# All blocks of two output projections in seven-product pairs, with the first pair's products in another order

## The chip, the cores and the metric

One NeuronCore of a Trainium2 chip runs the whole program. The time is the device time of one execution in microseconds, given as the median of several runs. The profile is one execution of the same program, taken by the hardware profiler. PE is the engine for matmuls, PEld its loading of weights, DVE the vector engine, ACT the scalar engine, POOL the general one, SP the queue that issues most of the DMAs.

## What is computed

The kernel is one inference step of a two-layer decoder for 576 tokens (512 of a prompt and 64 of eight samples) at a model width of 2048. All is float32, with each operand split into a rounded part and a rest, so that three matmuls make one product. The change concerns only the last line of each layer:

```python
def gla_layer(h, ...):          # first layer
    ...
    o = o.reshape(B, L, GLA_VALUE_DIM).astype(h.dtype) * jax.nn.silu(r)
    return h + o @ w_out, S.astype(s0.dtype)

def swa_layer(h, ...):          # second layer
    ...
    o = o.astype(h.dtype) * jax.nn.silu(z)
    return h + o @ w_out

# trunk: y = rmsnorm(h, g_final)
```

`o @ w_out` is a product of 576 x 2048 with 2048 x 2048, computed with features in the partitions and tokens in the columns.

## The kernel before

**Layout.** Activations lie in `HP[0..3]`, four rows of 128 features x 576 tokens each; `hpt(k)` is row k of 16. Before a projection they are split into `X[k]`, a rounded part and a rest of 576 columns each. The 576 columns are two halves of 288 (HT). Weights come in blocks of 128 output features x 2048 input features. They are loaded in tiles `raw` (eight groups of 128 input features, three buffers) and split in chunks of four groups into `wh` (a copy on ACT) and `wl` (a subtraction on DVE); four buffers each let the splits run up to four chunks ahead of PE (L166 to 175).

**Plain block** (`dense`, L185): 16 groups x 3 parts x 2 halves = 96 matmuls of 288 columns for one block of outputs.

**Pair** (`dense_pair`, L221): two blocks of outputs are made together. Inputs are divided into k < 8 and k >= 8, tokens into the two halves, which makes a 2 x 2 by 2 x 2 product of blocks with quarters x11, x12 (k < 8), x21, x22 (k >= 8). It is done with seven products instead of eight, by Winograd's form: 7 x 8 x 3 = 168 matmuls of 288 columns for what two plain blocks do with 192. The products are A, P4, P5, B, P6, P7, C (`PRODUCTS`, L217). Their inputs are x11, x21, x22, the differences t1 = x11 - x12 and t2, t3, t4 (`sums`, L258: t3 = x22 - x12, t2 = t3 + x11, t4 = t2 - x21, in groups g of two k each), and weights w11, w12, w22 and sums s1 to s4 of quarters. s1 and s3 are added by an accumulating DMA that POOL issues (L233); s2 and s4 are made in place from s1 on DVE (L241, L243). `pair_out` (L292) evacuates each product and puts the two output blocks together.

**Where t1 lies.** `XT` holds t2, t3, t4 in tiles of their own. t1 replaces x12: `first_sums` (L275) writes x11 - x12 over x12 in `HP`, and `split_half` (L281) splits it into the right halves of X[0..7]. A plain block needs x12 there, a pair needs t1.

**Stages.** `out_start` (L881) begins a projection: it splits all 16 rows, runs plain blocks (12 and 13 in the first layer, 12 in the second) with the last group of sums (`sums_hp(3)`) beside the first of them, then `first_sums`, and after the plain blocks the split of t1. Ahead of it the last gate blocks (`r_phase`, L376, and `z_phase`, L914) run with the groups 0 to 2 of sums beside them. X[k] is one tile for each k, so row k of the new input can be split only after the last gate block has read the old X[k]. The pairs follow: seven in the first layer, six (outputs 0 to 11) in the second.

**Tail of the second layer** (L1197 to 1253). Outputs 13, 14, 15 (`NB` = 3) are plain blocks again, in two parts of 320 and 256 columns, so that the final norm of the first part runs beside the second. They need x12 back in X: the second halves of rows 0 to 7 were stored to `dg2` by the gate phase and are read into unused rows of `HP[3]` (six) and a tile `st` (two) and split after the last pair. After each part come the sum of squares, the norm (`make_rstd`, `rstd_soon`), sixteen scalings on DVE (L1252) and sixteen stores (L1253).

**Order.** The kernel is built with `TileContext(nc, schedule_with_timeline_sim=True)` (L1359). The builder fixes the order of each engine's queue, with what stands earlier in the program first among what it takes to be ready. On the chip each queue runs in that order.

## Time and profile before

| | us |
|---|---|
| median of 3 runs (1757.25 to 1759.37) | 1758.03 |
| the profiled execution, its time | 1753.48 |
| the profiled execution, its span | 1751.70 |

| engine | busy us | share of the span |
|---|---|---|
| PE | 1729.3 | 99% |
| DVE | 1274.6 | 73% |
| ACT | 852.2 | 49% |
| POOL | 137.6 | 8% |

The share of busy time is an average over stages with different limits. What a change of one stage is worth is read in that stage: when its blocks end, and which engine is late. A row of the timeline is one instruction, or several of one kind that follow one another.

### The profile page before, as it was taken

How to read it: one execution, taken by the hardware profiler on the slowest of the kernel's cores; microseconds unless marked ns; L12 is line 12 of the kernel's file. 1: busy time of each engine (PE TensorE's matmuls, PEld its weight loads, DVE VectorE, ACT ScalarE, POOL GpSimd, SP SyncE). 2: the span in 40 equal slices, each digit the busy share in tenths (PEclk: the TensorE clock that was granted, in tenths of full speed). 3: DMA queues.
4: the chain of work that ended last, by engine and by line, in shares of the span. 5: the costliest groups of instructions: out<-in, count | busy, mean ns of one | idle time of the engine just before them, and what ended most of it. 6: DMA issues, size and time to landing. Idle time of an engine off the chain costs nothing.

```text
span 1751.7 us, 33967 instructions
## 1 busy us (share of the span) xinstructions
PE 1729.3 (99%) x12862; PEld 1709.6 (98%) x12862; DVE 1274.6 (73%) x2895; ACT 852.2 (49%) x1773; POOL 137.6 (8%) x216
## 2 busy tenths in 40 slices
PE   9999999999999999999999999999999999999997
PEld 9999999999999999999999999999999999999996
DVE  8567776777777787658777866787878755587774
ACT  7543334334334443435444655677767632364441
POOL 3000001001001000100121100100101000002210
PEclk9999999999999999999999999999999999999998
DMA  8345644565465344522677444343333252227643
GB/s 313 110 150 180 199 139 125 170 188 155 149 184 183 117 135 151 167 96 86 190 218 209 158 138 112 95 126 94 113 94 103 71 168 88 85 92 196 191 149 108
DMA packets 127123, 253.86 MB, mean 145 GB/s; under 512 B 23120, under 2 KB 52688, under 8 KB 126928
## 3 DMA queue, kind: packets, MB, share of 16 engines
q1 hardware_dynamic: 123216, 238.06, 42.9%
q0 software_dynamic: 3744, 13.63, 4.3%
q8 instruction: 101, 1.65, 0.4%
q14 instruction: 62, 0.51, 0.1%
HBM read 196.20 MB, written 44.83 MB: 138 GB/s over the span
## 4 chain that ended last, share of the span: by engine, by line
PE 93%; issue 2%; DMA 2%; DVE 2%; ACT 1%; SPq 0%; POOL 0%; POOLq 0%; DVEq 0%; ACTq 0%
PE pd L181 59%; PE pb L251 16%; PE pb L661 2%; PE pb L1076 1%; PE pb L747 1%; PE pd L469 1%; PE pb L836 1%; PE pb L1059 1%; PE pb L835 1%; PE pb L833 1%; PE pb L1058 1%; PE pb L748 1%; PE pb L1086 1%; PE pb L1087 1%; PE pb L679 1%
## 5 line engine op out<-in xcount | busy, mean ns | idle before, releaser
L181 PE MATMUL pd<-x,wh 128*128 128x288 f32 x5376 | 982.6, 298 | 0.0
L181 PEld LDWEIGHTS pd<-x,wh 128*128 128x128 f32 x5376 | 806.2, 189 | 7.1 <-ACT wh L169 0.3
L181 PE MATMUL pd<-x,wl 128*128 128x288 f32 x2688 | 591.5, 298 | 0.0
L169 ACT CAST wh<-raw 128x512 fp32r<-128x512 f32 x422 | 260.6, 618 | 401.2 <-PE pd L181 317.7
L181 PEld LDWEIGHTS pd<-x,wl 128*128 128x128 f32 x2688 | 437.6, 189 | 2.8
L170 DVE TENSOR_TENSOR wl<-raw,wh 128x512 fp32r<-128x512 f32 x422 | 303.4, 720 | 152.5 <-ACT wh L169 150.2
L251 PE MATMUL pb<-x,wh 128*128 128x288 f32 x832 | 166.7, 295 | 0.0
L251 PEld LDWEIGHTS pb<-x,wh 128*128 128x128 f32 x832 | 133.5, 188 | 0.0
L251 PE MATMUL pb<-t,wh 128*128 128x288 f32 x624 | 125.9, 296 | 0.7 <-ACT wh L169 0.6
L251 PE MATMUL pb<-x,wl 128*128 128x288 f32 x416 | 122.3, 295 | 0.0
L170 DVE TENSOR_TENSOR wl<-rs,wh 128x512 fp32r<-128x512 f32 x104 | 81.8, 791 | 32.4 <-ACT wh L169 30.2
L169 ACT CAST wh<-rs 128x512 fp32r<-128x512 f32 x104 | 64.0, 620 | 83.5 <-PE pb L251 76.2
L251 PEld LDWEIGHTS pb<-t,wh 128*128 128x128 f32 x624 | 100.3, 188 | 1.1 <-ACT wh L169 0.9
L251 PE MATMUL pb<-t,wl 128*128 128x288 f32 x312 | 92.5, 297 | 0.5 <-DVE wl L170 0.5
L251 PEld LDWEIGHTS pb<-x,wl 128*128 128x128 f32 x416 | 78.1, 188 | 0.0
L119 POOL TENSOR_TENSOR acc<-acc,st 128x576 f32<-128x576 f32 x46 | 71.0, 1542 | 81.3 <-ACT st L114 80.3
L117 POOL COPY acc<-st 128x576 f32<-128x576 f32 x7 | 6.3, 906 | 886.1 <-ACT st L114 797.7
L1068 ACT ACTIVATE s<-s,tiny 128x257 f32<-128x257 f32 (+1 forms) x128 | 61.1, 479 | 27.7 <-DVE tiny L1065 27.3
L815 ACT CAST sh<-Si 128x512 fp32r<-128x512 f32 x64 | 39.7, 620 | 66.5 <-PE pb L835 42.1
L114 ACT ACTIVATE st<-hp 128x576 f32<-128x576 f32 (+2 forms) x66 | 43.3, 663 | 43.9 <-DVE hp L1238 26.1
L251 PEld LDWEIGHTS pb<-t,wl 128*128 128x128 f32 x312 | 58.7, 188 | 0.9 <-DVE wl L170 0.9
L1065 DVE CUSTOM_DVE_ANT_0 s<-pb,distp,sinkp 128x256 f32<-128x256 f32 (+1 forms) x128 | 52.2, 447 | 7.1 <-PE pb L1059 6.1
(281 smaller groups left out, 2466.9 us busy)
## 6 DMA issues: line engine op xcount, KB each, us to landing
raw<-in_wA_dram SPq DMA_DIRECT2D x90, 512.0 KB
raw<-in_wB_dram SPq DMA_DIRECT2D x64, 512.0 KB
Si<-in_state_dram SPq DMA_DIRECT2D x64, 256.0 KB
out_gla_sample_dram<-Si SPq DMA_DIRECT2D x64, 256.0 KB
raw<-in_wOB_dram SPq DMA_DIRECT2D x26, 512.0 KB
raw<-in_wOA_dram SPq DMA_DIRECT2D x25, 512.0 KB
rs<-in_wOA_dram SPq DMA_DIRECT2D x14, 512.0 KB
rs<-in_wOA_dram POOLq DMA_DIRECT2D x14, 512.0 KB, 8.3
```

The costliest lines, as they stand in the source:

```text
L114: act(sq[:, lo:hi], src, AF.Square)
L119: self.eng.tensor_tensor(self.acc[:, lo:hi], self.acc[:, lo:hi], sq[:, lo:hi], ALU.add)
L169: nc.scalar.copy(wh, raw)
L170: vec.tensor_tensor(wl, raw, f32(wh), ALU.subtract)
L181: mm(p[:, a, :HT], w, x[:, part, a * HT:(a + 1) * HT], start=(k == 0 and w is wh and part == 0), stop=(k == KT - 1 and w is wl))
L251: mm(p, wt[:, kk, :], xpart(x, k, part), start=(opens and k == 0 and wt is wh and part == 0), stop=(k == 7 and wt is wl), skip_group_check ...
L469: mm(held[i][a][:, :HT], w[:, k % 4, :], X[k][:, part, a * HT:(a + 1) * HT], start=(k == 0 and w is wh and part == 0), stop=(k == KT - 1 a ...
L661: mm(p[:, o:o + N], keys(li)[:, f * 128:(f + 1) * 128], queries(li)[:, f, :], start=(f == 0), stop=(f == 1))
L679: mm(p[:, 0:N], k[:, f, :], qx[:, f, 0:N], start=(f == 0), stop=(f == 1))
L815: nc.scalar.copy(sh, Si)
L1065: vec.tensor_tensor_reduce(s[:, e, off:256], p[:, e * 256 + off:(e + 1) * 256], distp[:, off:256], slope(i), sinkp[:, i:i + 1], ALU.add, A ...
L1068: act(s[:, e, off:257], s[:, e, off:257], AF.Exp, scale=-1.0, bias=tiny[:, e:e + 1], accum_out=tiny[:, 2 + e:3 + e])
```

## The change

- `split_pairs` takes the place of `out_start`. For the k < 8 it makes x11 - x12 for two rows at once in a tile `st` and splits x11 and the difference as halves of X[k]; the rows k >= 8 are split whole. Then comes the last group of sums. There are no plain blocks; `HP` keeps x12.
- The first projection is eight pairs. The second is seven pairs, in the order 12, 0, 2, 4, 6, 8, 10, and its tail has two plain blocks (14 and 15) instead of three.
- `dense_pair` takes an order of products. The first pair of each projection runs `FIRST` (A, P5, B, P4, P6, P7, C); its loads are issued in the order in which this needs them.
- x12 comes back during the last pair (10): four halves are loaded into `HP[3]` ahead of it, four into two `st` tiles after product A, and all eight are split after product B.

```diff
@@ -218,14 +218,21 @@
                 "B": ("w12", "x21", 0, False), "P6": ("s2", "t2", 3, True), "P7": ("s3", "t3", 1, True),
                 "C": ("s4", "x22", 2, False)}
 
-    def dense_pair(wdram, blk, evac):
+    ORDER = ("A", "P4", "P5", "B", "P6", "P7", "C")
+
+    FIRST = ("A", "P5", "B", "P4", "P6", "P7", "C")
+
+    def dense_pair(wdram, blk, evac, order=ORDER):
 
         def quarter(b, hf):
             return wdram[blk + b, :, hf * 1024:(hf + 1) * 1024].rearrange("p (k n) -> p k n", n=128)
 
         raw = {}
-        for name, b, hf, more in (("w11", 0, 0, None), ("w22", 1, 1, None), ("s1", 1, 0, (1, 1)),
-                                  ("w12", 0, 1, None), ("s3", 1, 0, (0, 0))):
+        parts = {"w11": (0, 0, None), "w22": (1, 1, None), "s1": (1, 0, (1, 1)), "w12": (0, 1, None), "s3": (1, 0, (0, 0))}
+        for name in (PRODUCTS[n][0] for n in order):
+            if name not in parts:
+                continue
+            b, hf, more = parts[name]
             pool, tag = (wp, "raw") if more is None else (tpool[0], "rs")
             raw[name] = pool.tile([128, 8, 128], F32, tag=tag, name=nm(tag), bufs=3)
             dma(raw[name], quarter(b, hf))
@@ -233,7 +240,8 @@
                 nc.gpsimd.dma_start(raw[name], quarter(*more), accum_op=ALU.add)
         raw["s2"] = raw["s4"] = raw["s1"]
         banks = {}
-        for n, (w, x, b, opens) in PRODUCTS.items():
+        for n in order:
+            w, x, b, opens = PRODUCTS[n]
             if opens:
                 banks[b] = bank(b)[:, 0:HT]
             p = banks[b]
@@ -271,12 +279,6 @@
     def sums_hp(g):
         i = 2 * g % 4
         return sums(g, HP[g // 2][:, i:i + 2, :], HP[g // 2 + 2][:, i:i + 2, :])
-
-    def first_sums():
-
-        for h in range(2):
-            x12 = HP[h][:, :, HT:NT]
-            vec.tensor_tensor(x12, HP[h][:, :, 0:HT], x12, ALU.subtract)
 
     def split_half(k, src):
 
@@ -324,22 +326,16 @@
                     dma(dh1[j], hpt(j))
         return f
 
-    def out_pairs(wdram, js, src, ss, store):
+    def out_pairs(wdram, js, src, ss, store, also=None):
         for j in js:
             r1, r0 = resid(src(j + 1)), resid(src(j))
-            yield from dense_pair(wdram, j, pair_out(j, r0, r1, ss, store))
-
-    def out_block(wdram, j, src, ss, store):
-        r = resid(src(j))
-
-        def f(p):
-            if j % 4 == 0:
-                new_hp(j // 4)
-            vec.tensor_tensor(halves(hpt(j)), p, r, ALU.add)
-            ss.add(hpt(j))
-            if store:
-                dma(dh1[j], hpt(j))
-        yield from dense(wdram, j, f)
+            f = pair_out(j, r0, r1, ss, store)
+
+            def g(n, p):
+                f(n, p)
+                if also and j == js[-1]:
+                    also(n)
+            yield from dense_pair(wdram, j, g, FIRST if j == js[0] and not also else ORDER)
 
     bgs = []
 
@@ -878,18 +874,22 @@
             run(phase(range(a, a + 2)))
             drain()
 
-    def out_start(wdram, blks, src, ss, store):
-
-        for k in range(KT):
+    def split_pairs():
+
+        for g in range(4):
+            t1 = st().rearrange("p (a n) -> p a n", a=2)
+            i = 2 * g % 4
+            x = HP[g // 2][:, i:i + 2, :]
+            vec.tensor_tensor(t1, x[:, :, 0:HT], x[:, :, HT:NT], ALU.subtract)
+            for i in range(2):
+                k = 2 * g + i
+                o = new_x(k)[:, :, 0:HT]
+                nc.scalar.copy(o[:, 0, :], hpt(k)[:, 0:HT])
+                vec.tensor_tensor(o[:, 1, :], hpt(k)[:, 0:HT], f32(o[:, 0, :]), ALU.subtract)
+                split_half(k, t1[:, i, :])
+        for k in range(8, KT):
             split_plain(k, hpt(k))
-        bgs.append([sums_hp(3), 0.5, 0.0])
-        for j in blks:
-            run(out_block(wdram, j, src, ss, store))
-            if j == blks[0]:
-                drain()
-                first_sums()
-        for k in range(8):
-            split_half(k, hpt(k)[:, HT:NT])
+        finish(sums_hp(3))
 
     ssB = [None]
     with tc.tile_pool(name="lp", bufs=1) as lp:
@@ -900,8 +900,8 @@
         def x_row(j):
             return xT[j * 128:(j + 1) * 128, :]
 
-        out_start(A["wOA"], (12, 13), x_row, ss, True)
-        run(out_pairs(A["wOA"], (0, 2, 4, 6, 8, 10, 14), x_row, ss, True))
+        split_pairs()
+        run(out_pairs(A["wOA"], range(0, KT, 2), x_row, ss, True))
         ssB[0] = ss.acc
 
 
@@ -1194,31 +1194,38 @@
 
 
 
-    NB, NS = 3, 12
+    NB = 2
     ss = SumSq(nc.gpsimd)
     with tc.tile_pool(name="zp", bufs=1) as zp:
         tpool[0] = zp
         with_sums(z_phase, RS)
-        out_start(A["wOB"], (12,), lambda j: dh1[j], ss, False)
-        for j in range(0, NS, 2):
-            if j == NS - 2:
-
-                back = [HP[3][:, 1 + k // 2, k % 2 * HT:(k % 2 + 1) * HT] for k in range(6)]
-                for k in range(6):
+        split_pairs()
+
+
+        back = []
+
+        def x12_back(n):
+            if n == "A":
+                for _ in range(2):
+                    t = halves(st())
+                    back.extend([t[:, 0], t[:, 1]])
+                for k in range(4, 8):
                     dma(back[k], dg2[k])
-            run(out_pairs(A["wOB"], (j,), lambda j: dh1[j], ss, False))
-        t = halves(st())
-        for k in (6, 7):
-            dma(t[:, k - 6], dg2[k])
-            back.append(t[:, k - 6])
-        for k in range(8):
-            split_half(k, back[k])
+            elif n == "B":
+                for k in range(8):
+                    split_half(k, back[k])
+
+        run(out_pairs(A["wOB"], (12, 0, 2, 4, 6, 8), lambda j: dh1[j], ss, False))
+        for k in range(4):
+            back.append(HP[3][:, 2 + k // 2, k % 2 * HT:(k % 2 + 1) * HT])
+            dma(back[k], dg2[k])
+        run(out_pairs(A["wOB"], (10,), lambda j: dh1[j], ss, False, x12_back))
         ss.eng = vec
         rf = cp.tile([128, NT], F32, name="rstdF", tag="rstd")
         mhalf = cp.tile([128, 4], F32, name="mhalf", tag="mhalf")
         nc.gpsimd.memset(mhalf, -0.5)
         W, R = {}, {}
-        for j, tag in zip(range(KT - NB, KT), ("t4", "t2", "t3")):
+        for j, tag in zip(range(KT - NB, KT), ("t4", "t2")):
             W[j] = zp.tile([128, 2, KT, 128], F32R, tag=tag, name=nm("w"))
             R[j] = zp.tile([128, NT], F32, tag="rs", name=nm("r"), bufs=3)
             for hf in range(2):
```

## Rows read from the trace of the kernel before

**Rows 1.** The page's chain that ended last, shares of the span.
```profile
PE 93%; issue 2%; DMA 2%; DVE 2%; ACT 1%; SPq 0%; POOL 0%; POOLq 0%; DVEq 0%; ACTq 0%
```

**Rows 2.** Timeline of DVE, first projection: start us, us, what [idle before <-releaser]
```profile
791.04 0.76 DVE L381 SCALAR_TENSOR_TENSOR st<-pd,rstd 128x576 f32<-128x576 f32 x1 [1.40 <-PE pd L181]
...
807.06 0.75 DVE L381 SCALAR_TENSOR_TENSOR st<-pd,rstd 128x576 f32<-128x576 f32 x1
...
829.43 0.76 DVE L338 TENSOR_TENSOR hp<-pd,ld 128x576 f32<-128x576 f32 x1 [2.08 <-PE pd L181]
...
852.13 0.45 DVE L321 TENSOR_TENSOR hp<-pb,ld 128x288 f32<-128x288 f32 x1
...
874.44 0.44 DVE L321 TENSOR_TENSOR hp<-pb,ld 128x288 f32<-128x288 f32 x1
```

**Rows 3.** Timeline of DVE, evacuations around the second projection's front.
```profile
1534.23 0.76 DVE L919 SCALAR_TENSOR_TENSOR st<-pd,rstdB 128x576 f32<-128x576 f32 x1 [1.42 <-PE pd L181]
...
1550.18 0.75 DVE L919 SCALAR_TENSOR_TENSOR st<-pd,rstdB 128x576 f32<-128x576 f32 x1
...
1584.49 0.45 DVE L321 TENSOR_TENSOR hp<-pb,ld 128x288 f32<-128x288 f32 x1
...
1606.77 0.45 DVE L321 TENSOR_TENSOR hp<-pb,ld 128x288 f32<-128x288 f32 x1
```

**Rows 4.** Busy time by stretch; columns in the first line.
```profile
core 0: us, PE busy (x) PEld busy (x) DVE busy (x) ACT busy (x) POOL busy (x), PEclk, DMA share, GB/s
778.20:791.00 12.80, 12.80 (x99) 12.80 (x98) 9.29 (x13) 4.94 (x9) 0.00 (x0) 1.00 0.26 83
791.00:803.80 12.80, 12.80 (x99) 12.80 (x98) 12.60 (x19) 11.93 (x21) 0.00 (x0) 1.00 0.24 75
803.80:816.60 12.80, 12.80 (x99) 12.80 (x98) 11.73 (x18) 4.26 (x7) 0.00 (x0) 1.00 0.28 92
...
1534.20:1547.00 12.80, 12.80 (x98) 12.80 (x98) 12.62 (x19) 11.95 (x21) 0.00 (x0) 1.00 0.23 75
1547.00:1559.80 12.80, 12.80 (x98) 12.80 (x98) 11.29 (x19) 5.87 (x11) 0.00 (x0) 1.00 0.15 50
1559.80:1571.60 11.80, 10.67 (x76) 9.99 (x76) 11.25 (x19) 6.99 (x14) 0.88 (x1) 1.00 0.37 115
...
1740.00:1752.00 12.00, 0.90 (x4) 0.61 (x3) 6.36 (x16) 0.00 (x0) 0.00 (x0) 0.50 0.51 175
```

**Rows 5.** Timeline of DVE, one row of each kind of piece.
```profile
801.11 2.76 DVE L102 TENSOR_TENSOR x<-hp,x 128x576 fp32r<-128x576 f32 x4
...
807.73 1.29 DVE L170 TENSOR_TENSOR wl<-raw,wh 128x512 fp32r<-128x512 f32 x2
...
833.90 1.23 DVE L241 TENSOR_TENSOR rs<-rs,raw 128x1024 f32<-128x1024 f32 x1
...
1562.83 1.19 DVE L285 TENSOR_TENSOR x<-hp,x 128x288 fp32r<-128x288 f32 x3
```

**Rows 6.** Timeline of PE, waits at the start of the tail.
```profile
1701.40 0.56 PE L1236 MATMUL pd<-x,w 128*128 128x320 f32 x2 [0.55 <-ACT x L284]
1702.94 19.95 PE L1236 MATMUL pd<-x,w 128*128 128x320 f32 x141 [0.98 <-DVE x L285]
```

**Rows 7.** Timeline of DVE in the tail: evacuations and scalings.
```profile
1711.76 0.49 DVE L1238 TENSOR_TENSOR hp<-pd,r 128x320 f32<-128x320 f32 x1 [2.16 <-PE pd L1236]
...
1718.80 0.49 DVE L1238 TENSOR_TENSOR hp<-pd,r 128x320 f32<-128x320 f32 x1 [5.46 <-PE pd L1236]
...
1728.08 7.49 DVE L1252 SCALAR_TENSOR_TENSOR hp<-hp,c_vecs,rstdF 128x320 f32<-128x320 f32 x16
1735.49 0.42 DVE L1238 TENSOR_TENSOR hp<-pd,r 128x256 f32<-128x256 f32 x1
1736.37 0.42 DVE L1238 TENSOR_TENSOR hp<-pd,r 128x256 f32<-128x256 f32 x1 [0.47 <-PE pd L1236]
```

**Rows 8.** Timeline of PE in the tail, right parts.
```profile
1723.03 13.30 PE L1236 MATMUL pd<-x,w 128*128 128x256 f32 x109
```

## The prediction

> **What bounds the kernel now.** I read the chain of waits first: PE holds 93% of it [rows 1], so time is won by taking matmuls away as long as PE keeps being fed, and lost wherever PE begins to wait. Then I read the rhythm of the evacuations on DVE, because each stands at the end of a block. In the first output projection the evacuation of r block 14 starts at 791.04 and that of the second plain block at 829.43, both waiting on PE: three dense blocks in 38.39 us, 12.80 us each, 0.133 us for each of 96 matmuls. From the last evacuation of one pair to that of the next is 874.44 - 852.13 = 22.31 us for 168 matmuls, the same 0.133 us [rows 2]. So PE never waits there: the two plain blocks at the front cost only their matmuls. In the second projection the rhythm is broken: from 1534.23 two dense blocks (25.60) and a first pair (22.70, as 829.43 to 852.13 in the first projection) would end at 1582.53, and the row stands at 1584.49 [rows 2, 3]. With one plain block as cover the front already loses 1.96 us. The busy times of each stretch say why: PE is busy throughout, but for 1.1 us after 1559.8, and in the 25.6 us after 791.0 DVE is busy 12.60 + 11.73 = 24.33 us, 95%, and in the 37.4 us after 1534.2 it is busy 35.16 us, 94% [rows 4]. DVE is the second limit, at these two places alone, and the plain blocks lie there as its cover. The evacuation of r block 15, whose matmuls end at 791.04 + 12.80 = 803.84, comes only at 807.06 [rows 2]: DVE is 3 us behind already.
>
> **Change, part 1: matmuls.** First projection: two plain blocks go (25.60), an eighth pair comes (22.31): **-3.29 us** [rows 2]. Second projection: the plain block at its front goes (-12.80), a seventh pair comes (+22.31), and one of three blocks in the tail goes. How much of that last is worth anything is read in the tail (part 3).
>
> **Part 2: the two fronts.** What covered DVE is gone; what DVE must do is hardly less. Prices per piece, start to start within runs of the same form: 576 wide 0.67 us (four in 2.76, each 0.76 long), a weight split 0.60 (two in 1.29), a half 0.37 (three in 1.19), the sum of weights in place 1.23 [rows 5]. From the evacuation of the last block but one to the last weight split of the first pair DVE has: two gate evacuations of three pieces (6 x 0.67 = 4.0); four differences x11 - x12 (2.7), sixteen half splits in place of eight whole ones (5.9), eight whole splits (5.4); the last group of sums (6 x 0.67 = 4.0); fifteen weight splits (9.0); two sums of weights (2.5); six evacuation pieces of the products (5 x 0.37 + 0.67 = 2.5). Sum 36.0 us. PE has a dense block and a pair for it, 12.80 + 22.31 = 35.1 us, and its last chunk (12 matmuls, 1.6 us) comes after the last split.
> First projection: without any idle DVE would be ready at 791.04 + 36.0 = 827.0, PE at 828.6; unhindered PE would end at 803.84 + 22.31 = 826.15, so it loses 2.5 us. At the 95% of this very stretch it is 791.04 + 37.9 + 1.6 = 830.5, a loss of 4.4. Second projection: 1534.23 + 38.3 (94%) + 1.6 = 1574.1 against 1547.03 + 22.31 = 1569.34, a loss of 4.8; without idle 2.5.
> Two things move this. Downwards: the four differences need only rows of HP that are long done, and DVE is idle for 3.5 of the 12.8 us before 791.0 [rows 4]; if they go there, each front loses 2.7 less. Upwards: the queues are in order and their order is fixed when the kernel is built; in the second projection such an order cost 1.96 us even under cover, and may again, so up to 6.4 and 6.8. I take 4.4 and 4.8, the values at the busy share that the rows show. The new order of the first pair's products (P4 fourth, so that t4 of the last group, the end of the longest chain of sums, comes late) doesn't change DVE's total; it decides only which product waits. Against the old order it is worth at most the time of the two products moved ahead, 2 x 24 x 0.133 = 6.4 us, and costs at least nothing; the sum above has it in.
> Loads: a pair reads seven quarters of weights where two plain blocks read four. In the stretches named DMA has room (shares 0.15 to 0.37 [rows 4]), and a weight tile of the first pair comes free when r15's splits free it, before 800, so I put the loads of w11, w12, w22 and both residuals at nothing; were that cover gone, one would cost a late product, about 1 us. On POOL's queue come two more accumulating loads in each projection; nothing but the sums of squares stands behind them: nothing.
>
> **Part 3: the tail of the second projection.** After the last pair come the plain blocks, left part (320 columns) of each, then right part (256). One left part takes 1718.80 - 1711.76 = 7.04 us [rows 7], a right one 48 x 13.30/109 = 5.9 [rows 8]. The last left part is evacuated at 1718.80; then come its norm and sixteen scalings on DVE (1728.08 to 1735.57), and behind them in DVE's queue the evacuations of right parts, at 1735.49 and, waiting for PE, at 1736.37. The end hangs on this last one. DVE is free 16.7 us after 1718.80, PE 17.6 us after it: even now they are within 0.9 us. With two blocks PE needs 2 x 5.9 + 0.3 (the norm's matmul) = 12 us there, DVE the same 16.7. So the tail gains 0.88 us behind the last left part, not 5.9, and 7.04 ahead of it. From evacuation to the end (15.3 us) nothing changes.
> To the last left part: -12.80 + 22.31 - 7.04 = **+2.47**; behind it **-0.88**; the old loss at the front goes, **-1.96**; x12's return, which now runs during the last pair, takes away the two waits of PE for its splits, 0.55 + 0.98 = **-1.53** [rows 6]. Its loads: four are issued ahead of the last pair and four behind product A, on SP's queue, ahead of the tail's weights; two of three st tiles are held for them. The first product that follows takes the third, and POOL has freed the others a product earlier. Nothing, or at most the 1.5 us again (a split late for the tail); I take 0.4.
>
> **Sum.** Fixed: -3.29 + 2.47 - 0.88 - 1.96 - 1.53 = -5.2. New waits: 4.4 + 4.8 + 0.4 = 9.6. Together **+4.4 us**, on the profiled execution (span 1751.70, time 1753.48) 1757.9. The median shown is 1758.03, 4.55 above it; I carry that over: **1762.4 us**. 0.2% is 3.5 us, about what a measurement of this kernel can tell from no change.
>
> **Rivals.** (a) *Faster:* DVE's idle time ahead of 791.0 and 1534.2 takes all differences, and PE fills what waits remain with products whose inputs are done (P6 and P4 need the last group of sums only for k = 6 and 7). For: PE mixed blocks in the tail of before. Against: those products need weight splits, which are DVE's too. With 0.6 us for each front: 1.2 - 5.2 = -4.0, **1754.0**. It decides if DVE's backlog at the pair's end is under 1 us. (b) *The differences alone go early:* 1.7 + 2.1 + 0.4 - 5.2 = -1.0, **1757.0**. (c) *The last evacuation is queued ahead of scalings that are still waiting:* the tail becomes PE's, 16.7 - 12 = 4.7 less, **1757.7**. Against: the row at 1735.49, a right part done some 6 us before the next, stands behind all sixteen. (d) *The queues' order costs as in the old second front:* 6.4 + 6.8 + 1.5 - 5.2 = +9.5, **1767.5**. (e) *TensorE's clock:* it is granted 0.50, its 1.2 GHz level, in 1740 to 1752, after PE ran out of work, and 1.00 in 1559.8 to 1571.6 with 1.1 us of waiting [rows 4]. If a front's wait brings it down, a product at half rate costs 24 x 0.133 = 3.2 more at each front, +6.4: **1768.8**. The Trainium skill (TensorE: Matmul & The Clock Gate, "Why this matters for your kernels") warns that pauses between bursts of matmuls bring the half rate back; by that rule this change is worse than its sum, and the row at 1740 agrees with it for a long pause. No row here shows a pause of 2 to 4 us.
>
> **Chances.** Forecast 0.42 (its own range 1759.5 to 1765.5), a 0.11, b 0.25, c 0.07, d 0.09, e 0.06. Range **1755.0 to 1768.0**: it leaves out most of a, e and the upper end of d. Faster by over 0.2% (below 1754.5): 0.11. Slower (above 1761.5): two thirds of the forecast, d, e and a little of b: 0.46. Within: 0.43.
>
> **What would show it.** Right: PE has waits of 2 us and more in all within the first pair of each projection, released by DVE or ACT (weight splits, differences, t4), and DVE at 95% from 791 on; the first pair's last evacuation stands near 831 and 1574.5 instead of 826.5 and 1569.7; later pairs keep 22.31; in the tail DVE runs its sixteen scalings straight into the last evacuation, without a wait on PE, 16.7 us behind the last left part. Wrong: the first pairs last under 24 us; the differences stand ahead of 791; or the last evacuation still waits on PE. The granted clock under 1.00 in a first pair would speak for e.

## The result, and the profile after

| | us |
|---|---|
| kernel before, median of 4 (1756.80 to 1759.37) | 1757.64 |
| changed kernel, median of 4 (1767.47 to 1770.91) | 1768.37 |
| ratio, 95% interval | 1.0070 (1.0058 to 1.0081) |
| changed kernel, the profiled execution: time, span | 1770.91, 1769.1 |

By the medians the change costs 10.7 us, by the ratio 12.3 (10.2 to 14.2), where +4.4 was forecast. The direction is the forecast one, the size is more than double, and the time lies 0.4 us above the upper end of the range.

The page's busy times and its chain of the changed kernel hardly differ from those of before [rows 1]:

```profile
PE 1731.0 (98%) x12814; PEld 1709.4 (97%) x12814; DVE 1285.8 (73%) x2924; ACT 856.6 (48%) x1786; POOL 140.6 (8%) x221
...
PE 93%; DVE 2%; issue 2%; DMA 2%; ACT 0%; SPq 0%; POOL 0%; POOLq 0%; DVEq 0%; ACTq 0%
```

These shares say nothing of the loss; it has to be read in the rhythm of the evacuations. DVE's timeline of the changed kernel, first front (L377 and L381 are the first and the last piece of a gate evacuation, L883 a difference x11 - x12, L287 the rest of a half split, L323 the last evacuation of a pair):

```profile
794.28 0.76 DVE L377 SCALAR_TENSOR_TENSOR st<-pd,rstd 128x576 f32<-128x576 f32 x1 [1.40 <-PE pd L181]
...
807.75 0.75 DVE L377 SCALAR_TENSOR_TENSOR st<-pd,rstd 128x576 f32<-128x576 f32 x1
...
809.01 0.75 DVE L883 TENSOR_TENSOR st<-hp 128x576 f32<-128x576 f32 x1
...
813.42 0.81 DVE L381 SCALAR_TENSOR_TENSOR hp<-hp,c_vecs,st 128x576 f32<-128x576 f32 x1
814.15 2.09 DVE L883 TENSOR_TENSOR st<-hp 128x576 f32<-128x576 f32 x3
816.16 0.76 DVE L102 TENSOR_TENSOR x<-hp,x 128x576 fp32r<-128x576 f32 x1
816.83 2.30 DVE L287 TENSOR_TENSOR x<-st,x 128x288 fp32r<-128x288 f32 x6
...
860.94 0.45 DVE L323 TENSOR_TENSOR hp<-pb,ld 128x288 f32<-128x288 f32 x1
```

and the second front, where L919 and L923 are the pieces of the gate evacuation:

```profile
1545.26 0.76 DVE L919 SCALAR_TENSOR_TENSOR st<-pd,rstdB 128x576 f32<-128x576 f32 x1 [1.42 <-PE pd L181]
...
1559.98 0.76 DVE L883 TENSOR_TENSOR st<-hp 128x576 f32<-128x576 f32 x1
...
1564.40 0.75 DVE L923 TENSOR_TENSOR hp<-hp,st 128x576 f32<-128x576 f32 x1
1565.07 2.09 DVE L883 TENSOR_TENSOR st<-hp 128x576 f32<-128x576 f32 x3
...
1611.87 0.45 DVE L323 TENSOR_TENSOR hp<-pb,ld 128x288 f32<-128x288 f32 x1
```

From the evacuation of gate block 14 to the last one of the second pair lie one dense block (12.80), a first pair (22.70) and a pair (22.31): 57.81 us if PE never waits [rows 2]. What a kernel needs beyond that is called its **front loss** from here on. It is 860.94 - 794.28 - 57.81 = **8.85 us** in the first projection and 1611.87 - 1545.26 - 57.81 = **8.80 us** in the second. The forecast had 4.4 and 4.8. The rows say where: the first difference starts at 809.01, the other three at 814.15, directly behind the last piece of gate block 15's evacuation. These differences are `t1`, which P5, the second product in the new order, reads. PE's timeline shows that it waits for these pieces one after the other:

```profile
811.17 0.40 PE L259 MATMUL pb<-x,wh 128*128 128x288 f32 x1 [0.96 <-ACT x L286]
...
813.20 0.40 PE L259 MATMUL pb<-x,wh 128*128 128x288 f32 x1 [1.63 <-DVE x L287]
...
815.42 0.61 PE L259 MATMUL pb<-x,wh 128*128 128x288 f32 x1 [1.05 <-ACT x L286]
...
817.34 0.61 PE L259 MATMUL pb<-x,wh 128*128 128x288 f32 x1 [1.30 <-DVE x L287]
```

Busy times by stretch (columns as in [rows 4]) show what else happens there:

```profile
807.10:819.90 12.80, 7.86 (x41) 6.74 (x40) 12.80 (x24) 6.65 (x16) 0.00 (x0) 0.76 0.13 41
810.00:813.00 3.00, 0.60 (x3) 0.19 (x1) 3.00 (x5) 1.28 (x3) 0.00 (x0) 1.00 0.10 27
813.00:816.00 3.00, 1.75 (x6) 1.12 (x6) 3.00 (x6) 1.73 (x5) 0.00 (x0) 0.61 0.46 147
816.00:819.00 3.00, 1.70 (x8) 1.67 (x8) 3.00 (x8) 1.56 (x6) 0.00 (x0) 0.50 0.00 0
819.00:822.00 3.00, 3.00 (x19) 3.00 (x19) 2.83 (x5) 1.07 (x2) 0.00 (x0) 0.75 0.03 5
```

In these 12.80 us DVE has no idle time at all, and PE is idle for 4.94 us. Behind the first two of the four waits the granted clock falls: it is 0.61 in 813 to 816, 0.50, the 1.2 GHz level, in 816 to 819, and 0.75 in 819 to 822.

The tail, DVE and then PE (L1245 evacuations, L1259 scalings), to be laid beside [rows 7]:

```profile
1737.09 0.49 DVE L1245 TENSOR_TENSOR hp<-pd,r 128x320 f32<-128x320 f32 x1 [5.45 <-PE pd L1243]
...
1746.37 7.49 DVE L1259 SCALAR_TENSOR_TENSOR hp<-hp,c_vecs,rstdF 128x320 f32<-128x320 f32 x16
1753.78 0.42 DVE L1245 TENSOR_TENSOR hp<-pd,r 128x256 f32<-128x256 f32 x1
...
1754.76 1.01 PE L149 MATMUL pb<-ones,st 128*128 128x1 f32 x4 [5.47 <-ACT st L1250]
```

From the last left part to the last evacuation it takes 1753.78 - 1737.09 = 16.69 us, with the evacuation straight behind the scalings and PE without work: as forecast.

**Where the time came from.** From gate block 14 of the first projection to that of the second: 750.98 us here, 743.19 before [rows 2, 3], +7.79. Of this -3.29 are matmuls and +8.85 the front loss; 2.2 are left; they lie between the projection's last pair and gate block 14 of the second projection, in stages that the change doesn't touch (as do the 3.2 us by which 794.28 is later than 791.04, ahead of the first projection). From gate block 14 of the second to the last evacuation: 208.52 here, 202.14 before [rows 3, 7], +6.38. That is +8.80 - 1.96 (the old loss) + 2.47 - 0.88, and -2.05, a remainder, which is put down to x12's return. The changed stretches alone make 7.79 - 2.2 + 6.38 = **+11.9 us**, which the interval of the ratio holds.

### The profile page after: what moved, and what is told of

Read it like the earlier page. It is cut to its first block, busy times and chain, and to the rows that moved or that the text cites. A ratio compares the mean times of both kernels' runs of the same rounds, so it can differ in the third digit from the quotient of the medians.

```text
span 1769.1 us, 33949 instructions
## 1 busy us (share of the span) xinstructions
PE 1731.0 (98%) x12814; PEld 1709.4 (97%) x12814; DVE 1285.8 (73%) x2924; ACT 856.6 (48%) x1786; POOL 140.6 (8%) x221
## 4 chain that ended last, share of the span: by engine, by line
PE 93%; DVE 2%; issue 2%; DMA 2%; ACT 0%; SPq 0%; POOL 0%; POOLq 0%; DVEq 0%; ACTq 0%
PE pd L181 57%; PE pb L259 18%; PE pb L657 2%; PE pd L465 2%; PE pb L1076 1%; PE pb L743 1%; PE pb L1059 1%; PE pb L829 1%; PE pb L1058 1%; PE pb L832 1%; PE pb L744 1%; PE pb L831 1%; PE pb L1086 1%; PE pb L1087 1%; PE pb L465 1%
## 5 line engine op out<-in xcount | busy, mean ns | idle before, releaser
L181 PE MATMUL pd<-x,wh 128*128 128x288 f32 x5184 | 949.9, 299 | 0.0
L181 PEld LDWEIGHTS pd<-x,wh 128*128 128x128 f32 x5184 | 778.6, 189 | 7.1 <-ACT wh L169 0.3
L181 PE MATMUL pd<-x,wl 128*128 128x288 f32 x2592 | 571.3, 298 | 0.0
L181 PEld LDWEIGHTS pd<-x,wl 128*128 128x128 f32 x2592 | 422.7, 189 | 2.8
L259 PE MATMUL pb<-x,wh 128*128 128x288 f32 x960 | 197.0, 300 | 9.8 <-DVE x L287 5.8
L259 PEld LDWEIGHTS pb<-x,wh 128*128 128x128 f32 x960 | 156.6, 191 | 12.4 <-DVE x L287 6.9
L259 PE MATMUL pb<-t,wh 128*128 128x288 f32 x720 | 144.5, 296 | 0.0
L259 PE MATMUL pb<-x,wl 128*128 128x288 f32 x480 | 142.9, 299 | 1.0 <-DVE wl L170 1.0
L259 PEld LDWEIGHTS pb<-t,wh 128*128 128x128 f32 x720 | 115.6, 188 | 0.0
L259 PE MATMUL pb<-t,wl 128*128 128x288 f32 x360 | 106.2, 297 | 0.0
```

What stands on the lines that cost most here:

```text
L181: mm(p[:, a, :HT], w, x[:, part, a * HT:(a + 1) * HT], start=(k == 0 and w is wh and part == 0), stop=(k == KT - 1 and w is wl))
L259: mm(p, wt[:, kk, :], xpart(x, k, part), start=(opens and k == 0 and wt is wh and part == 0), stop=(k == 7 and wt is wl), skip_group_check ...
```

## The experiments

The front losses of all kernels are read in the same way, from the evacuation of gate block 14 to the last one of the second pair. "Sum" is the forecast's fixed part (-5.2; -3.29 and -1.9 where one projection is changed) and the losses; "measured" is the ratio's excess with its interval, in us. Each loss is read from one profiled execution. Of the edits only the main lines are shown; `...` marks what is left out.

| kernel | front 1 | loss | front 2 | loss | sum | measured |
|---|---|---|---|---|---|---|
| changed kernel | 794.28 to 860.94 | 8.85 | 1545.26 to 1611.87 | 8.80 | +12.5 | +12.3 (10.2 to 14.2) |
| differences in place | 793.15 to 855.75 | 4.79 | 1538.09 to 1601.77 | 5.87 | +5.5 | +3.7 (1.9 to 5.6) |
| with filler matmuls | 793.33 to 859.14 | 8.00 | 1540.74 to 1606.33 | 7.78 | +10.6 | +10.4 (7.7 to 13.2) |
| first projection only | 792.41 to 860.30 | 10.08 | as before | | +6.8 | +7.4 (4.7 to 10.0) |
| second projection only | as before | | 1534.98 to 1602.36 | 9.57 | +7.7 | +6.7 (4.6 to 8.8) |
| old order of products | 795.53 to 862.10 | 8.76 | 1547.95 to 1613.93 | 8.17 | +11.7 | +13.7 (10.7 to 16.8) |
| in place, fewer rests | 790.86 to 851.28 | 2.61 | 1534.68 to 1594.36 | 1.87 | -0.7 | +0.9 (-0.9 to 2.6) |
| in place, rests on GpSimd | 791.46 to 857.64 | 8.37 | 1540.20 to 1606.57 | 8.56 | +11.7 | +12.5 (10.2 to 14.9) |

Every sum lies inside its interval, so the losses account for the time. The same first front, with DVE's pieces in the same order, lost 8.85 us in the changed kernel and 10.08 in the run with the first projection only; the second front lost 8.80 and 9.57. So a difference of 1 us between two of these losses needs a reason seen in the rows. Two theories stood at the start. **S**: the differences stand too late, because each needs an `st` tile; there are three, the last gate block's evacuation takes two of them, and the differences queue behind it. **D**: as the prediction had it, DVE's total sets the loss, wherever the pieces stand. The clock was a third.

**Differences in place.** Groups 0 to 2 are written over x12 (nothing reads it any more once their sums are done), so they need no `st` tile; group 3 still does.

```diff
-            t1 = st().rearrange("p (a n) -> p a n", a=2)
             i = 2 * g % 4
             x = HP[g // 2][:, i:i + 2, :]
+            t1 = x[:, :, HT:NT] if g < 3 else st().rearrange("p (a n) -> p a n", a=2)
```

> The changed kernel, but the differences x11 - x12 of groups 0 to 2 are written over x12 in HP, so they need no st tile; only group 3 still takes one. Theory S (in the changed kernel the differences wait for an st tile that the evacuation of the last gate block gets first): the differences now run before that evacuation, the waits of PE in product P5 of both first pairs (0.96 + 1.63 + 1.05 + 1.30 us and 0.97 + 1.62 + 0.96 + 1.30 us) all but go, the granted clock stays at 1.00 there, and each front loses about 2 us instead of 8.8: 1755 to 1758. Theory D (DVE's whole work in the front decides, wherever the differences stand): only the 2.7 us of differences per front move, each front still loses 4 to 5 us: 1761 to 1764.

Measured: 1760.26 us (10 runs) against 1756.03, ratio 1.0021 (1.0011 to 1.0032), an excess of 3.7 us. Both expectations were reckoned from 1757.6 (as +5.5 and 1763.2 are below); as excesses they are +3.4 to +6.4 for D and -2.6 to +0.4 for S, so the time is D's. DVE's timeline (first two rows below), a stretch of the busy times and PE's timeline of this kernel:

```profile
784.84 0.75 DVE L883 TENSOR_TENSOR hp<-hp 128x576 f32<-128x576 f32 x1
...
809.54 0.74 DVE L883 TENSOR_TENSOR st<-hp 128x576 f32<-128x576 f32 x1
...
805.90:818.70 12.80, 11.29 (x81) 10.60 (x80) 12.73 (x21) 6.33 (x13) 0.00 (x0) 1.00 0.23 72
...
813.34 0.40 PE L259 MATMUL pb<-t,wl 128*128 128x288 f32 x1 [1.32 <-DVE wl L170]
```

The differences without a tile run ahead of gate block 14's evacuation (793.15; the row at 784.84 is the last of the three); only the fourth waits. PE has 11.29 busy of 12.80 us where it had 7.86, the clock stays at 1.00, and its longest wait at each front is now for a weight split (1.32 and 1.48 us), DVE's last and largest item. The same pieces in another place are worth 4.06 us at the first front and 2.93 at the second, the half clock included: S explains that part, and the fourth difference, which still needs a tile, is its control. The rows don't show why the differences weren't put into 798 to 807 in the changed kernel, between the evacuations of gate blocks 14 and 15, when neither held a tile; only that those which need none stand early. What is left, 4.79 and 5.87, looks like the prediction's 4.4 and 4.8 but is more than D: three of four differences (2.0 us) are out of the front now, and D's own sum without them is about 2.4 and 2.8. At the second front 1568 to 1574, where the clock is granted at 0.77 around waits of 0.28 us for a group of sums and 1.48 us for a weight split, has a share in it. More buffers for `st`, the direct test of S, were not tried.

**Filler matmuls.** The changed kernel with 34 matmuls into an unused bank ahead of P5's pieces in each first pair, so that PE isn't idle there. On PE's queue they stand as 27 ahead of P5's first matmul and 7 behind it.

```diff
+                        fill = {(0, 0): 7, (0, 1): 11, (2, 0): 7, (2, 1): 9}.get((k, part), 0)
+                        if order is FIRST and n == "P5" and wt is wh and fill:
+                            if k == 0 and part == 0:
+                                spare = bank(3)[:, 0:HT]
+                            for _ in range(fill):
+                                mm(spare, XT["t3"][:, 0, 0, 0:128], X[0][:, 0, 0:HT], start=True, stop=True)
```

> The changed kernel with 34 further matmuls of 288 columns, whose result nobody reads, in front of product P5's first matmuls of each first pair (27 ahead of the first, 7 before its second), 4.5 us at full clock, in a time in which PE waits anyway. Theory C (PE's pause brings the clock to half, and part of the front's loss is that half clock): the granted clock stays at 1.00, the waits stay as sums, and each front gives back about 3 us although PE has more to do: 1761 to 1764. Rival (the waits alone make the loss, the low clock falls into time that DVE needs anyway): no change, 1767 to 1770, or worse by what fillers delay.

Measured: 1765.66 us (4 runs) against 1756.03, ratio 1.0059 (1.0044 to 1.0075). Busy times and PE's one long wait in the first front of this kernel:

```profile
806.00:812.00 6.00, 6.00 (x47) 6.00 (x46) 6.00 (x10) 3.04 (x7) 0.00 (x0) 1.00 0.06 17
812.00:818.00 6.00, 4.49 (x33) 4.15 (x32) 6.00 (x13) 3.25 (x9) 0.00 (x0) 1.00 0.22 73
...
816.38 0.40 PE L265 MATMUL pb<-x,wh 128*128 128x288 f32 x1 [1.51 <-DVE x L293]
```

The clock is granted in full at both fronts, and the losses fall only from 8.85 and 8.80 to 8.00 and 7.78. The last wait for a half of `t1` ends just as far behind gate block 14 as in the changed kernel (23.05 us against 23.06, 22.97 against 22.99 at the second front), so the fillers delay nothing there, and the half clock of the changed kernel's trace is worth about 0.85 and 1.0 us. By the times alone the two kernels can't be told apart: +10.4 (7.7 to 13.2) and +12.3 (10.2 to 14.2).

**One projection at a time.** The first as changed and the second as before, and the other way round.

> Only the first projection is changed (eight pairs, new front); the second is that of the kernel before, with its plain block, six pairs and three tail blocks. By the rhythm in the two profiles the first projection costs 8.8 us of front loss against 3.3 us of matmuls saved: +5.5, 1763.2. If the difference between the two kernels came from elsewhere (the second projection alone, or stages that the change does not touch), it would be 1757.6 or 1754.3.

Measured: 1762.45 us (5 runs) against 1756.03, ratio 1.0042 (1.0027 to 1.0057). Its front lost 10.08 us where the changed kernel's lost 8.85. The busy times of this kernel say why:

```profile
817.00:820.00 3.00, 3.00 (x15) 3.00 (x14) 2.82 (x5) 1.20 (x3) 0.00 (x0) 0.50 0.03 5
```

The last wait for `t1` ends 23.06 us behind gate block 14 here too, but then the clock stays at 0.50 for a stretch in which PE is busy all the time: 15 matmuls in 3.00 us, where the changed kernel got through 19 at 0.75 in 819 to 822. Set against the run with fillers, the half clock cost 2.1 us in this trace, and 1.8 in the second front of the run below.

> The first projection as in the kernel before, the second as changed: the complement of the run with the first projection only. By the changed kernel's trace its front loses 8.8 us; with the fixed terms of the second projection (+2.47 - 0.88 - 1.96 - 1.53 = -1.9) this gives +6.9 us on the kernel before, and a front loss of 8 to 9 us. If the two projections hurt each other (a slower clock or a later queue carried from the first to the second), it is less: +4 or under, with a front loss under 7 us.

Measured: 1761.91 us (7 runs) against 1755.05, ratio 1.0038 (1.0026 to 1.0050). The two excesses add up to 0.0080, the whole change has 0.0070 (0.0058 to 0.0081) and, in the run with the old order below, 0.0078: no carrying over from one projection into the other shows; with these intervals one of under some 4 us would not.

**Old order of products.** The changed kernel with A, P4, P5, B, P6, P7, C in the first pairs too.

```diff
-            yield from dense_pair(wdram, j, g, FIRST if j == js[0] and not also else ORDER)
+            yield from dense_pair(wdram, j, g, ORDER)
```

> The changed kernel with the first pairs in the order of the kernel before (A, P4, P5, B, P6, P7, C) and nothing else undone. It measures what the reordering is worth. The prediction gave it between 0 and 6.4 us a front (two products of 24 matmuls moved ahead). Theory W (the queue order of PE is planned by what is ready, so products mix and the written order matters little): within 1.5 us of the changed kernel, that is +10 to +12 us on the kernel before. Theory O (P4 stands in front of P5 and B on PE and waits for the last group of sums, done at 827 in the changed kernel): each front loses 3 to 6 us more, so +16 to +23 us on the kernel before, with a wait of PE of over 4 us in a row released by DVE's sums (t).

Measured: 1768.38 us (4 runs) against 1754.64, ratio 1.0078 (1.0061 to 1.0096). PE's timeline of its first front has one long wait where the changed kernel has four shorter ones, for the same splits:

```profile
815.54 0.40 PE L259 MATMUL pb<-x,wh 128*128 128x288 f32 x1 [0.88 <-ACT x L286]
...
819.19 0.50 PE L259 MATMUL pb<-x,wh 128*128 128x288 f32 x1 [3.25 <-DVE x L287]
...
830.42 0.41 PE L259 MATMUL pb<-t,wh 128*128 128x288 f32 x1 [0.69 <-DVE t L276]
```

The losses, 8.76 and 8.17, are those of the new order, where theory O had 3 to 6 us more for each; the time, +13.7 (10.7 to 16.8), lies between the two theories and can't decide. By the losses the reordering is worth nothing that these runs can tell: theory W. P4 doesn't stand in the way: the part of it whose sums are done (18 matmuls with `t`, 811.29 to 813.69) runs ahead of P5, the rest behind, and the last group of sums costs only 0.69 us of waiting.

**In place, with 5.4 us less for DVE.** The differences in place, and the rests of rows k >= 8 aren't made: this run leaves them out, and the matmuls that read them take the rounded parts.

```diff
         for k in range(8, KT):
-            split_plain(k, hpt(k))
+            nc.scalar.copy(new_x(k)[:, 0, :], hpt(k))
...
```

> As the run with differences in place, with 8 DVE instructions less at each front: the rests of rows k >= 8 are not made (the matmuls that read them in pairs and tail read the rounded parts instead, so that PE has the same work). It leaves out that part of the computation. 8 x 0.67 = 5.4 us of DVE go at each front. Theory D (with the differences early, DVE's total sets what is left of the loss, 4.8 and 5.9 us): both losses go to 0.5 or less, the run is 8 to 10 us below the run with differences in place, about 5 us below the kernel before. Rival O (what is left is the order of the queues and the chain of the last gate block): the losses stay over 3 us each, the run is less than 4 us below the run in place.

Measured: 1756.05 us (10 runs) against 1754.64, ratio 1.0005 (0.9995 to 1.0015). PE's waits in its first front, and ACT's split that ends the second of them:

```profile
810.82 0.40 PE L259 MATMUL pb<-t,wl 128*128 128x288 f32 x1 [0.57 <-DVE wl L170]
...
820.20 0.54 PE L259 MATMUL pb<-x,wh 128*128 128x288 f32 x2 [0.62 <-ACT wh L169]
...
819.53 0.62 ACT L169 CAST wh<-rs 128x512 fp32r<-128x512 f32 x1 [0.97 <-PE pb L259]
```

The losses fall from 4.79 and 5.87 to 2.61 and 1.87. Neither theory's number holds: D had 0.5 or less, its rival over 3. Of 5.4 us taken off DVE 2.2 and 4.0 come back (at the second front the half clock of the run in place goes too). So DVE's total does set a part of what is left once the differences are early. By D's sum nothing should be left here, and 2.61 and 1.87 are. The rows show where: from matmul to matmul, against the pace of 0.133 us, PE loses 0.84 us at the first of these waits, 1.20 at the second and 0.50 at 824.1, together 2.54 of the 2.61. These are waits for weight splits, and ACT itself stood idle for 0.97 us ahead of its split at 819.53 until PE released it, by its row; that would be for one of the four `wh` buffers, a second ring. No run here tests that, so the cause of this part stays open.

**The rests on GpSimd.** The differences in place; nothing is left out, GpSimd makes the rests of rows k >= 8.

```diff
-            split_plain(k, hpt(k))
+            t = new_x(k)
+            nc.scalar.copy(t[:, 0, :], hpt(k))
+            nc.gpsimd.tensor_tensor(t[:, 1, :], hpt(k), f32(t[:, 0, :]), ALU.subtract)
```

> As the run with differences in place, with the eight rests of rows k >= 8 made on GpSimd instead of DVE; nothing is left out. By theory D it takes 5.4 us off DVE at each front; if GpSimd's subtractions don't slow DVE and end before product B needs them, it comes near the run without these rests: 1751 to 1754. If GpSimd is slow (over 1.5 us for each, 12 us in all) B and the accumulating loads behind them in its queue are late: 1758 to 1764.

Measured: 1767.31 us (4 runs) against 1754.64, ratio 1.0071 (1.0058 to 1.0085): worse than both expectations, as bad as the change itself. GpSimd's timeline, DVE's beside it, and PE's:

```profile
799.43 13.85 POOL L893 TENSOR_TENSOR x<-hp,x 128x576 fp32r<-128x576 f32 x7 [61.62 <-ACT x L892]
...
805.78 1.99 DVE L883 TENSOR_TENSOR st<-hp 128x576 f32<-128x576 f32 x1
807.69 2.46 DVE L249 TENSOR_TENSOR rs<-rs,raw 128x1024 f32<-128x1024 f32 x1
810.07 1.95 DVE L380 SCALAR_TENSOR_TENSOR st<-st,st 128x576 f32<-128x576 f32 x1
811.94 1.88 DVE L170 TENSOR_TENSOR wl<-raw,wh 128x512 fp32r<-128x512 f32 x1
...
814.25 0.40 PE L259 MATMUL pb<-x,wh 128*128 128x288 f32 x1 [4.32 <-DVE x L287]
```

GpSimd subtracts at 1.98 us for each of seven. The four pieces of DVE beside it take 1.99, 2.46, 1.95 and 1.88 us where they took 0.75, 1.22, 0.75 and 0.69 in the changed kernel: 1.2 us more for each. What was taken off DVE came back as slower work. The fourth difference itself stands earlier than in the run in place, 14.32 us behind gate block 14's evacuation against 16.39, but the split of it, for which PE waits, comes 22.29 us behind it against 20.06.

**A tail of two blocks.** The kernel before with its third tail block moved to the second front (plain blocks 12 and 13 there, 14 and 15 in the tail).

```diff
-    NB, NS = 3, 12
+    NB, NS = 2, 12
...
-        out_start(A["wOB"], (12,), lambda j: dh1[j], ss, False)
+        out_start(A["wOB"], (12, 13), lambda j: dh1[j], ss, False)
...
```

> The kernel before with block 13 of the second projection moved from the tail to the front (plain blocks 12 and 13 there, six pairs, two tail blocks); the number of matmuls is the same. Theory T (behind the last left part DVE's norm and sixteen scalings decide, not PE): the moved block costs 12.8 us ahead and gives back 7.04 + 0.88 in the tail, and the front with two plain blocks loses nothing where it lost 1.96: +2.9, 1760.5, with the last evacuation 16.7 us behind the last left part and no wait on PE. Rival (a tail block is worth its matmuls): 12.8 for 12.8 and the front's 1.96 gained, 1755.7, with the last evacuation waiting for PE 12 us behind the last left part.

Measured: 1756.55 us (10 runs) against 1756.03, ratio 1.0004 (0.9994 to 1.0013). DVE's tail:

```profile
1723.35 0.49 DVE L1239 TENSOR_TENSOR hp<-pd,r 128x320 f32<-128x320 f32 x1 [2.23 <-PE pd L1237]
...
1732.63 7.49 DVE L1253 SCALAR_TENSOR_TENSOR hp<-hp,c_vecs,rstdF 128x320 f32<-128x320 f32 x16
1740.04 0.41 DVE L1239 TENSOR_TENSOR hp<-pd,r 128x256 f32<-128x256 f32 x1
```

16.69 us again behind the last left part, set by DVE: the third block's right part was worth 0.88 us there, as the prediction worked out. The total, +0.7 (-1.1 to 2.3), is lower than the theory's +2.9 and above the rival's -1.96; from gate block 14 to the last evacuation the traces have 203.64 us against 202.14, +1.5. The theory had already counted the old loss of 1.96 us. What it left out is that PE's waits at the tail's start fall from 0.55 + 0.98 us to 0.45.

**The tail's columns 192 and 384.** The run above with the narrow part first, and the norm of the second part in four pieces of columns in place of three.

```diff
-        for lo, hi in ((0, 320), (320, NT)):
+        for lo, hi in ((0, 192), (192, NT)):
...
```

> The run with a tail of two blocks (one more plain block at the second front, tail blocks 14 and 15), with the tail's columns divided 192 and 384 instead of 320 and 256. Theory T (behind the last left part DVE's norm and scalings set the end, PE has slack): the left parts shrink by 2 x 48 x 128 columns, about 5 us by 7.04 us for 320 columns; behind the last left part PE takes over, 2 x 48 matmuls of 384 columns, about 17 us against 16.7; the last sixteen scalings and stores grow by 1 to 2 us. Sum -2.5 to -3.5 us on the run with 320 and 256 columns, so 1752.5 to 1754.5 where the kernel before has 1756.0. Rival (the stores of 384 columns set the end): no gain, 1756 or more.

Measured: 1753.71 us (11 runs) against 1754.64, ratio 0.9996 (0.9987 to 1.0005). DVE's tail:

```profile
1716.08 0.36 DVE L1239 TENSOR_TENSOR hp<-pd,r 128x192 f32<-128x192 f32 x1 [3.90 <-PE pd L1237]
...
1733.07 0.56 DVE L1239 TENSOR_TENSOR hp<-pd,r 128x384 f32<-128x384 f32 x1 [1.34 <-PE pd L1237]
```

Now the last evacuation waits for PE, 16.99 us behind the last left part: the balance has tipped to PE, as expected. Counted from gate block 14, the left parts end 4.3 us sooner than in the run above; the stretch behind the last evacuation grows by 2.0 us (17.3 against 15.4): -2.1 us by the traces where -2.5 to -3.5 was expected, and no difference from the kernel before that the runs can tell.

**x12's return alone.** The kernel before with this one part: loads ahead of the last pair and behind its product A, splits behind B.

```diff
...
+        def x12_back(n):
+            if n == "A":
+                t = halves(st())
+                for k in (6, 7):
+                    dma(t[:, k - 6], dg2[k])
+                    back.append(t[:, k - 6])
+            elif n == "B":
+                for k in range(8):
+                    split_half(k, back[k])
...
```

> The kernel before with one part of the change: x12's halves are loaded and split during the last pair (six into rows of HP[3] ahead of it, two into an st tile behind product A, all eight split behind product B). The prediction gave this part -1.53 us (two waits of PE, 0.55 and 0.98) and up to +0.4 for splits or loads that come late. Theory R: both waits of PE at the start of the tail go, 1.0 to 1.5 us below the kernel before. Rival: the eight splits delay the last pair's own weight splits on DVE or ACT, or hold an st tile that the pair needs: no gain, with waits of PE of 1 us in all inside the last pair.

Measured: 1752.86 us (12 runs) against 1755.05, ratio 0.9987 (0.9976 to 0.9997). DVE's timeline, gate block 14 of the second layer and the last evacuation:

```profile
1536.65 0.76 DVE L925 SCALAR_TENSOR_TENSOR st<-pd,rstdB 128x576 f32<-128x576 f32 x1 [1.42 <-PE pd L181]
...
1736.68 0.42 DVE L1248 TENSOR_TENSOR hp<-pd,r 128x256 f32<-128x256 f32 x1 [0.46 <-PE pd L1246]
```

200.03 us against 202.14 before [rows 3, 7]: -2.1 us, more than the two waits of [rows 6]. PE doesn't wait once from the last pair to the last left part. This part of the change is a gain by itself, and the only kernel here whose interval lies below the kernel before, if narrowly: 0.13% (0.03% to 0.24%).

## Why the prediction was wrong in size

By its own steps, in the traces:

| step | forecast | trace |
|---|---|---|
| new waits, first front | +4.4 | +8.85 |
| new waits, second front | +4.8 | +8.80 |
| new wait for x12's splits | +0.4 | 0 |
| x12's waits that go | -1.53 | -2.05 |
| matmuls, old loss, two-block tail | -3.66 | -3.66 |
| sum | +4.4 | +11.9 |

- **The step that failed is part 2.** It added up DVE's pieces, 36.0 us, took 95% for the busy share, and let the pieces stand in any order. The prices held, and so did the sum; busy times of the first front (columns as in [rows 4]), the first pair's last weight split and its last evacuation in the changed kernel:

```profile
794.28:830.00 35.72, 30.78 (x212) 29.66 (x211) 33.87 (x57) 22.10 (x43) 0.00 (x0) 0.90 0.14 46
...
832.03 0.68 DVE L170 TENSOR_TENSOR wl<-rs,wh 128x512 fp32r<-128x512 f32 x1
...
838.23 0.46 DVE L323 TENSOR_TENSOR hp<-pb,ld 128x288 f32<-128x288 f32 x1
```

  DVE is busy for 33.87 of 35.72 us, 95%, and ends its last split 38.4 us behind gate block 14's evacuation, where 37.9 was forecast. But PE isn't 1.6 us behind that, as forecast: the pair's last evacuation comes 5.5 us after the split. What failed is the order. The 1.6 us rested on PE keeping up with DVE's pieces as they come, and PE had stood idle for 4.94 us in 807.1 to 819.9. The prediction said that "the four differences need only rows of HP that are long done", and that was so, but they also need a tile to be written to. Three of them came behind the last gate block's evacuation, and PE stood still for P5 while DVE did work that was needed later. The prediction looked for what the new instructions read and didn't look for where they write. Of the 8.85 and 8.80 us the place of the differences makes 4.06 and 2.93 (0.85 and 1.0 of that, by the run with fillers, through the clock), DVE's amount of work 2.2 and 4.0 of the rest, and 2.61 and 1.87 stay open. These are differences of single traces.
- **Rival (b)** had the differences go early and priced the fronts at 1.7 and 2.1. With three of four early they cost 4.79 and 5.87: going early is possible, but not enough. Rival (a), 0.6 a front, wasn't reached even with 5.4 us less for DVE to do (2.61 and 1.87).
- **Rival (d)**, an order of the queues that costs 6.4 and 6.8, is the nearest to what happened, in its time (1767.5) and in its kind. But its price came from the old second front, where PE waited 0.63 and 0.46 us for weight splits and not for the differences; the new fronts lost 8.85 and 8.80.
- **Rival (e)**, the clock: it did fall to 0.50, behind waits of 0.96 and 1.63 us with 0.60 us of PE work in 810 to 813, where the prediction spoke of one pause of 2 to 4 us. By the run with fillers it costs 0.85 and 1.0 us in the changed kernel's trace, and 2.1 and 1.8 in the runs with one projection, not 3.2: a part of the half clock lay over a stretch where PE had only 1.70 of 3.00 us to do, and that part cost nothing. The Trainium skill (TensorE: Matmul & The Clock Gate, "Why this matters for your kernels") warns of pauses between bursts of matmuls; the rows agree that the clock falls, and the run with fillers says that it was not the main part.
- **The reordering** was given 0 to 6.4 us; no worth of it shows here, and PE's rows have the products mixed in either order.
- **The tail** was right in its mechanism and its size: 16.69 us against 16.7, with DVE's scalings straight ahead of the last evacuation.
- **x12's return** was undersized by some 0.5 us: [rows 6] counts the two waits, but the two matmuls between them take 0.56 us where the pace of a left part (7.04 us for 48) gives 0.29, so a wait's row isn't all of its cost. The forecast's +0.4 for late splits didn't come about: no wait of PE is left there.

## What to carry to other kernels

Before an instruction is counted as free to move, look at what it writes as well as at what it reads: an instruction that needs a tile of a small ring can stand in the queue behind the chain that takes the ring's tiles first. A total of work per engine gives the loss only where the pieces can stand in the order in which they are needed; where the engine is busy to the end, price the one chain that the other engine waits for. Work that covers a busy engine may look like waste (two plain blocks cost 3.3 us more than a pair) and be cheaper than the waits that it hides.

## What the hardware showed beside this

- In the changed kernel PE waited 0.96 and 1.63 us with 0.60 us of work in 810 to 813, and the granted clock went from 1.00 to 0.50 behind them; two more waits, of 1.05 and 1.30 us, followed. The run in place, with waits of 1.32 and 0.20 us in 805.9 to 818.7, kept 1.00.
- How long the clock then stays low can differ between two kernels with the same order of work at this place: 0.75 and 19 matmuls in 819 to 822 of the changed kernel, 0.50 and 15 in 817 to 820 of the run with the first projection only, both just behind the last wait. The fronts differ by 1.2 us.
- DVE was slower beside GpSimd: a 128x576 subtraction on DVE took 1.99 us beside GpSimd's, 0.75 alone; seven of GpSimd's took 13.85. The Trainium skill (SBUF — State Buffer, "SBUF: two separate sides") says that a GpSimd operation that reads SBUF and a DVE operation with two inputs from SBUF share a pair of ports and that the later one waits for the whole of the other; that four pieces of DVE with two inputs from SBUF, of 0.69 to 1.22 us alone, each take the same 1.2 us more here agrees with a wait of that kind.
